# Value products over all 128 columns, narrow products kept in whole groups, bias strips through DRAM and a shorter reciprocal root in a two-block forward pass

## The chip, the cores and the metric

The kernel runs on one core of a Trainium2 chip. The metric is the device time of one execution in microseconds (us); of three runs the median counts. The engines are TensorE (PE in the profile, with PEld for its weight loads), VectorE (DVE), ScalarE (ACT), GpSimd (POOL) and SyncE (SP), which here only issues transfers. ACT issues transfers too, and such an issue stands in ACT's own stream of instructions.

## The reference

256 tokens of width 1024 pass through two blocks of two layers each. The change touches the attention of the first block:

```
diff heads (4, two maps each):  p = softmax(q k / 8 + bias, causal);  a = p0 - lam * p1;  out = a @ v  (v: 128 wide)
moba heads (8, one own block):  p = softmax(q k / 8 + bias, causal);  out = p @ v                       (v: 64 wide)
bias[i, j] = rel_bias[bucket(i - j), head]      # depends on i - j alone
rms_norm(x) = x / sqrt(mean(x * x) + 1e-6) * g   # in both blocks, of x, q, k and the heads' outputs
```

The second block (gated linear attention, attention, convolution, gates) uses the same root and the same sums of squares, and six parts of its modulation (a vector times a 1024 x 3072 matrix) are computed by TensorE with 32 wide products inside the stages of the first block.

## The kernel before, in words

Activations lie transposed, 128 channels on the partitions and 256 tokens along the free axis. Each weight arrives from DRAM as `raw` tiles of 128 x 1024 and is split by ACT into `wH` (rounded to the matmul's fp32r) and by DVE into `wL` (the rest). A projection is three fp32r products (high by high, high by low, low by high), 256 columns each in block one. The plain fp32 products of the sums and of the attention weights with the values stand as two records each in the trace.

Nothing is issued in the order in which it is written. `Rec.record` (line 212) notes each operation with its dependences, and `Rec.order` (line 271) plays them through with a cost and a latency per operation and fixes the order for every engine. At each step it takes the engine that can start first, and on it the ready operation that was written first. All instructions therefore carry line 442, where they are emitted, and tiles are told apart by name.

The parts that the change touches:

- `gsum` (line 621) adds up squares over the partitions: up to four products of 32 output columns, each on its own 32 partitions of one PSUM tile (`ms<-xsq`, `ms<-qsq`, `ms<-osq`, `ms<-gsq`, `ms<-ksq`). `mod_part` (line 688) uses two such groups of four, of 512 columns, on the modulation weights (`x<-wada,cs`). `nc.after` makes all of a group ready at the same moment, but another operation that becomes ready may still be put between them.
- `rsqrt` (line 598) computes 1/sqrt on DVE from a shifted integer start and three Newton steps: 12 dependent instructions on tiles of 1 to 16 columns (`s<-s`), 13 where a scale follows. There are 42 of them.
- `bias_strips` (line 755) makes `brow`, 12 heads by 384 distances, in SBUF. `bias_strip` (line 768) spreads the row of each head over the partitions, shifted by one per partition, into a `strip` tile: 12 transfers of 128 KB issued by ACT, each reading from one partition of `brow` in 128 runs of 1 KB.
- `attn_scores` (line 815) adds the strip to the scores (`sb<-x,s,strip` on DVE), takes the row maximum and the exponential with its sum.
- `moba_pair` (line 971) handles two 64 wide heads per tile `a`: it transposes the weights (`x<-ck,sb`), copies them (`at` on ACT) and multiplies with the head's own 64 columns of `v`. Both heads' results lie in one PSUM tile `po`, head 0 on partitions 0 to 63 and head 1 on 64 to 127, and one ACT and one DVE instruction split `po` into `Y` (`y<-x`). `x` in the trace is any PSUM tile of the attention.

`attention1` runs two diff pairs and two moba pairs per layer. Each pair needs its scores' operand `ks`, which comes from a chain: squares, `gsum`, root, a spread copy (`wide`), transposes on PE, `k` on DVE, `ks` on ACT and DVE. PE executes its instructions in the fixed order, so a `x<-ks,qh` whose `ks` is late stops all that stands behind it.

Of the kernel before, what the change touches and what calls it, by code (L numbers as in the profile page):

```python
# [20 lines left out]
P = 128  # L21
# [6 lines left out]
NEG = -1.0e30  # L28
MAGIC = 0x5F3759DF
AHEAD = {"ps": 12, "T": 16, "Q": 14}  # L30
ROLES = {"mm": 4, "x4": 4, "ms": 3, "raw": 4, "H": 7, "L": 7, "ada": 4}
# [43 lines left out]
class Op:  # L75
    __slots__ = ("i", "eng", "fn", "args", "kw", "cost", "lat", "prio", "deps", "succ", "nd", "ready", "start", "end",
                 "new", "uses", "dma", "table", "alloc")

# [53 lines left out]
class Rec:  # L132


    def __init__(self, tc):
        self.tc, self.nc = tc, tc.nc
        nc = tc.nc
        self.vector, self.scalar, self.tensor = _Proxy(self, "DVE", nc.vector), _Proxy(self, "ACT", nc.scalar), _Proxy(self, "PE", nc.tensor)
        self.gpsimd, self.sync = _Proxy(self, "POOL", nc.gpsimd), _Proxy(self, "SP", nc.sync)
        self.ops, self.tiles, self.caps, self.psum, self.acc, self.role = [], {}, {}, set(), {}, {}  # L140
        self.seen, self.old = {}, set()
        self.offset = 0.0
        self.ahead, self.rolecap = {}, {}
        self.after = None

    def pool(self, ctx, name, bufs, **k):
# [16 lines left out]
    def box(self, ap):  # L163
        pat = ap.ap
        ps, pn = pat[0]
        ps = ps or 1
        p0, f0 = divmod(ap.offset, ps) if pn > 1 or ps > 1 else (0, ap.offset)
        f1 = f0 + 1
        for s, c in pat[1:]:
            f1 += s * (c - 1)  # L170
        return p0, p0 + pn, f0, f1
# [40 lines left out]
    def record(self, eng, method, fn, args, kw):  # L212
        o = Op()
        o.i, o.eng, o.fn, o.args, o.kw = len(self.ops), eng, fn, args, kw
        o.prio = o.i + self.offset
        out = kw["out"] if "out" in kw else args[0]
        outs = [out] + ([kw["accum_out"]] if kw.get("accum_out") is not None else [])
# [53 lines left out]
    def order(self):  # L271
# [74 lines left out]
        done = 0  # L346
        total = len(ops)
        while done < total:
            best = None
            for e in engs:  # L350
                t0 = t_eng[e]
                while future[e] and future[e][0][0] <= t0:
                    r, p, i = heapq.heappop(future[e])
                    heapq.heappush(avail[e], (p, i))
                if avail[e]:
# [9 lines left out]
            s, e = best  # L365
            t_eng[e] = max(t_eng[e], s)
            while future[e] and future[e][0][0] <= s:
                r, p, i = heapq.heappop(future[e])
                heapq.heappush(avail[e], (p, i))
            p, i = heapq.heappop(avail[e])  # L370
            o = ops[i]
# [43 lines left out]
            for j in o.succ:  # L415
# [8 lines left out]
                if q.nd == 0:  # L424
                    push(q)
            for tn in o.uses:
                left[tn] -= 1
# [20 lines left out]
class Emit:  # L448
# [149 lines left out]
    def rsqrt(self, src, n, scale=None, shape=None, guard=None, more=None):  # L598
        nc = self.nc
        tiles = [self.small(n) for _ in range(5)] + [self.small(n, I32)]  # L600
        v, y, t, u, r, h = tiles
        sh = (lambda q: q) if shape is None else (lambda q: q.rearrange(shape[0], **shape[1]))
        bits = lambda q, dt: q.bitcast(dt)
        if more is not None:
# [11 lines left out]
        if scale is not None:  # L616
            nc.vector.tensor_scalar(r, y, scale, None, ALU.mult)
            return tiles[4]
        return tiles[1]
# [68 lines left out]
    def mod_part(self, l, part, after):  # L688
# [4 lines left out]
        for kk in range(0, KT, 2):  # L693
# [5 lines left out]
            if kk % 4:  # L699
                nc.after = nc.last(raw)  # L700
                for g in range(4):
                    nc.tensor.matmul(ps[32 * g:32 * g + 32, :], self.cs[:, kk - 2 + g, :], ws[g], start=kk < 4, stop=kk >= 4)
                nc.after = None
                ws = []
# [50 lines left out]
    def bias_strips(self):  # L755
# [9 lines left out]
        self.strip = [None] * 6  # L765
        self.brow = row

    def bias_strip(self, i, after):

        nc = self.nc  # L770
        st = self.t2("strip")
        nc.after = after
        for a in range(2):
            src = self.brow[2 * i + a:2 * i + a + 1, 0:T]
# [3 lines left out]
        self.strip[i] = st.rearrange("p (a b) -> p a b", a=2)  # L778

# [35 lines left out]
    def attn_scores(self, pr, a, qg, kn, rq, rcol, head):  # L815
# [10 lines left out]
        for m in range(2):  # L826
# [5 lines left out]
            for t in range(2):  # L832
                nk = P * (t + 1)
                sl = slice(t * P, t * P + nk)
                nc.vector.scalar_tensor_tensor(sb[:, sl], ps[:, t * T:t * T + nk], rq[:, rcol(m, t):rcol(m, t) + 1],
                                               st[:, T - nk:T], ALU.mult, ALU.add)
                nc.vector.tensor_reduce(mx[:, t:t + 1], sb[:, sl], AX.X, ALU.max, negate=True)
# [133 lines left out]
    def moba_pair(self, pr, qg, kn, r, v, Y):  # L971
        nc = self.nc
        for a in range(2):
# [3 lines left out]
            for m in range(2):  # L977
# [4 lines left out]
                at = self.attn_transpose(s)  # L982
                o = po[m * 64:(m + 1) * 64, :]
# [833 lines left out]
def constants():  # L1817
# [30 lines left out]
    for lv in range(7):  # L1848
# [3 lines left out]
        masks[:, lv, :] = (seg[:, None] == seg[None, :]) & (half[:, None] != half[None, :])  # L1852
    return {"ck": ck, "oneh": oneh.astype(np.float32), "maskr": np.ascontiguousarray(maskr.astype(np.float32)),
            "masks": masks.reshape(P, 7 * P).astype(np.float32)}
# [25 lines left out]
```

## Time and profile before

| | us |
|---|---|
| median of 3 runs (2056.23 to 2058.48) | 2057.44 |
| the profiled execution | 2054.4 |
| its span, first to last instruction | 2052.6 |
| PE busy (share of the span) | 2027.0 (99%) |
| PEld busy | 1847.7 (90%) |
| DVE busy | 1464.4 (71%) |
| ACT busy | 1167.6 (57%) |
| mean DMA rate | 143 GB/s |

The profile is of one execution. A PE record's length overlaps the next record's, so the cost of a piece of PE work is read from the starts in the timeline: a 256 column fp32r product follows the one before after 0.12 us. Waits name the engine and tile that came last by the profile.

### The profile page before, as it was taken

Reading aid. Unit: us, or ns where it says so; the run is one execution under the profiler, and the core shown is the slowest. Engines: PE = TensorE matmul, PEld = TensorE weight load, DVE = VectorE, ACT = ScalarE, POOL = GpSimd, SP = SyncE. Lnnn points to the kernel's source line nnn. Section 1 sums busy time; section 2 is a strip of 40 time slices with the busy share of each in tenths; the row PEclk is TensorE's granted clock in tenths of the full one; section 3 lists DMA queues with packets and bytes.
Section 4 is the critical chain, followed back from the end, with each engine's and each line's share of the span. In section 5 each row is a group of like instructions: output and inputs, shape, how many; then the busy total and the mean of one; then the engine's idle time right before and its main releaser. Section 6 shows DMA issues by size and latency. Waiting matters only on the chain.

```text
span 2052.6 us, 35592 instructions
## 1 busy us (share of the span) xinstructions
PE 2027.0 (99%) x14158; PEld 1847.7 (90%) x14158; DVE 1464.4 (71%) x2846; ACT 1167.6 (57%) x2055; POOL 8.7 (0%) x20
## 2 busy tenths in 40 slices
PE   9989999999999999999999999999999999999998
PEld 7879999989999989988888888888888999999997
DVE  7778986888866699983477755563467888696663
ACT  6656656767665767762366323333357777575542
POOL 0000000000000000000000000000000000000000
PEclk9999999999999999999999999999999999999999
DMA  9765665555555121232122543342361225436551
GB/s 296 140 166 200 225 226 174 185 175 175 206 185 196 60 74 64 72 120 86 53 72 72 193 135 122 115 140 96 135 214 67 89 83 186 141 116 215 176 190 68
DMA packets 86846, 292.68 MB, mean 143 GB/s; under 512 B 9452, under 2 KB 17176, under 8 KB 86424
## 3 DMA queue, kind: packets, MB, share of 16 engines
q1 hardware_dynamic: 81544, 281.50, 39.6%
q10 hardware_dynamic: 5136, 8.91, 2.8%
q8 instruction: 111, 1.82, 0.4%
q14 instruction: 55, 0.45, 0.1%
HBM read 282.51 MB, written 4.19 MB: 140 GB/s over the span
## 4 chain that ended last, share of the span: by engine, by line
PE 97%; DMA 1%; DVE 1%; ACT 0%; issue 0%; ACTq 0%; SPq 0%; DVEq 0%
PE mm L442 78%; PE x L442 11%; PE acc L442 6%; PE ms L442 2%; DMA strip<-brow 1%; DVE s L442 0%; DMA xx<-in_xt_dram 0%; ACTq L442 0%; ACT h L442 0%; DVE wL L442 0%; DVE sb L442 0%; ACT y L442 0%; ACT wH L442 0%; ACT xg L442 0%; DVE h L442 0%
## 5 line engine op out<-in xcount | busy, mean ns | idle before, releaser
L442 DVE TENSOR_TENSOR wL<-raw,wH 128x1024 fp32r<-128x1024 f32 (+1 forms) x472 | 569.7, 1217 | 307.0 <-PE mm L442 144.6
L442 ACT ACTIVATE wH<-raw 128x1024 fp32r<-128x1024 f32 (+1 forms) x472 | 491.5, 1053 | 252.2 <-DVE wL L442 112.0
L442 PE MATMUL mm<-h2H,wH 128*128 128x256 f32 (+1 forms) x1504 | 504.2, 338 | 2.1 <-ACT h2H L442 2.1
L442 PE MATMUL mm<-h2L,wH 128*128 128x512 f32 (+2 forms) x1504 | 504.0, 337 | 0.0
L442 PE MATMUL mm<-h2H,wL 128*128 128x256 f32 (+1 forms) x1472 | 497.5, 338 | 0.0
L442 PEld LDWEIGHTS mm<-h2H,wH 128*128 128x128 f32 x1504 | 283.6, 190 | 33.2 <-issue 3.5
L442 PEld LDWEIGHTS mm<-h2L,wH 128*128 128x128 f32 (+1 forms) x1504 | 283.2, 189 | 28.7 <-issue 1.6
L442 PEld LDWEIGHTS mm<-h2H,wL 128*128 128x128 f32 x1472 | 279.3, 190 | 28.6 <-issue 1.0
L442 PE MATMUL mm<-h,wH 128*128 128x256 f32 x1216 | 219.6, 283 | 0.0
L442 PEld LDWEIGHTS mm<-h,wH 128*128 128x128 f32 x1216 | 189.6, 192 | 0.0
L442 PE MATMUL mm<-h,wL 128*128 128x256 f32 x608 | 172.0, 283 | 0.0
L442 PE MATMUL mm<-xg,wH 128*128 128x256 f32 x704 | 133.9, 289 | 1.5 <-ACT wH L442 1.5
L442 PE MATMUL acc<-hid,wH 128*128 128x256 f32 x704 | 128.2, 284 | 0.0
L442 PEld LDWEIGHTS mm<-h,wL 128*128 128x128 f32 x608 | 116.7, 192 | 0.0
L442 PEld LDWEIGHTS mm<-xg,wH 128*128 128x128 f32 x704 | 112.1, 195 | 4.0 <-ACT wH L442 1.9
L442 PE MATMUL mm<-xL,wH 128*128 128x512 f32 (+1 forms) x320 | 111.4, 348 | 0.0
L442 PE MATMUL mm<-xH,wL 128*128 128x512 f32 (+1 forms) x320 | 111.2, 348 | 0.0
L442 PE MATMUL mm<-xH,wH 128*128 128x512 f32 (+1 forms) x320 | 111.0, 348 | 0.0
L442 PEld LDWEIGHTS acc<-hid,wH 128*128 128x128 f32 x704 | 109.8, 192 | 0.8 <-issue 0.8
L442 PE MATMUL mm<-xg,wL 128*128 128x256 f32 x352 | 101.6, 290 | 0.2 <-DVE wL L442 0.2
L442 PE MATMUL acc<-hid,wL 128*128 128x256 f32 x352 | 98.4, 283 | 0.0
L442 ACT ACTIVATE gt<-mm,hb 128x512 f32<-128x512 f32 (+1 forms) x48 | 27.8, 579 | 116.1 <-PE mm L442 116.0
(295 smaller groups left out, 3850.5 us busy)
## 6 DMA issues: line engine op xcount, KB each, us to landing
raw<-in_w_dram SPq DMA_DIRECT2D x272, 512.0 KB, 3.7
raw<-in_w1up_dram SPq DMA_DIRECT2D x88, 512.0 KB, 4.1
wada<-in_wada_dram SPq DMA_DIRECT2D x48, 512.0 KB, 5.4
raw<-in_w1in_dram SPq DMA_DIRECT2D x46, 512.0 KB, 5.9
raw<-in_w1dn_dram SPq DMA_DIRECT2D x44, 512.0 KB, 4.4
raw<-in_w1out_dram SPq DMA_DIRECT2D x16, 512.0 KB, 4.5
crow<-in_crow_dram SPq DMA_DIRECT2D x6, 512.0 KB, 6.4
qh<-qh SPq DMA_DIRECT2D x16, 128.0 KB, 2.2
```

Source lines behind the costliest of these rows:

```text
L442: o.fn(*o.args, **o.kw)
```

## The change

1. `moba_pair`: the product of a head's weights takes the values of both heads, 128 columns, into its own half of `po`'s free axis, and the 64 rows of the head itself are read. The one ACT and one DVE instruction per tile become two each, on 64 partitions.
2. `gsum` and `mod_part` mark all but the first product of a group with `join`. When `order` has placed an operation and the next one in the text is so marked and ready, it is placed at once, whatever else is ready.
3. `bias_strips` stores `brow` to a DRAM tile by SP. `bias_strip` is one transfer by SP for two heads, 256 KB, 256 runs of 1 KB read from DRAM with a step of one element per partition. The constant tables are mirrored for that, and `attn_scores` reads the strip backwards, with a step of -1.
4. `rsqrt`: no shift (the halving is a product with -0.5 on the integer read as a number), one third-order step and one Newton step, with the scale folded in: 9 instructions.

```diff
     def gsum(self, ps, sqs, ones, start=True, stop=True):
         nc.after = max(nc.last(sq) for sq in sqs)
         for g, sq in enumerate(sqs):
+            nc.join = g > 0
             nc.tensor.matmul(ps[32 * g:32 * g + 32, :self.free(sq)], self.c(ones), sq, start=start, stop=stop)
-        nc.after = None
+        nc.after, nc.join = None, False
...
+            if must is not None:
+                e, i = ops[must].eng, must
+                p, s = ops[i].prio, max(t_eng[e], ops[i].ready)
+                gone.add(i)
+                must = None
...
+            if o.i + 1 < total and ops[o.i + 1].join and ops[o.i + 1].nd == 0:
+                must = o.i + 1
...
-        nc.vector.tensor_scalar(h, bits(tiles[0], I32), 1, None, ALU.logical_shift_right)
-        nc.vector.tensor_scalar(bits(tiles[1], I32), h, -1, MAGIC, ALU.mult, ALU.add)
-        for i in range(3):
-            nc.vector.tensor_tensor(out=t, in0=y, in1=y, op=ALU.mult)
-            nc.vector.scalar_tensor_tensor(u, t, -0.5, v, ALU.mult, ALU.mult)
-            nc.vector.scalar_tensor_tensor(y, u, 1.5, y, ALU.add, ALU.mult)
+        nc.vector.tensor_scalar(y.bitcast(I32), v.bitcast(I32), -0.5, MAGIC, ALU.mult, ALU.add)
+        nc.vector.tensor_tensor(out=t, in0=y, in1=y, op=ALU.mult)
+        nc.vector.tensor_tensor(out=w, in0=t, in1=v, op=ALU.mult)
+        nc.vector.scalar_tensor_tensor(w, w, RQ[1], w, ALU.add, ALU.mult)
+        nc.vector.scalar_tensor_tensor(y, w, RQ[2], y, ALU.add, ALU.mult)
+        nc.vector.tensor_tensor(out=t, in0=y, in1=y, op=ALU.mult)
+        nc.vector.scalar_tensor_tensor(w, t, -0.5 * f * RQ[0] ** 2, v, ALU.mult, ALU.mult)
+        nc.vector.scalar_tensor_tensor(r, w, 1.5 * f, y, ALU.add, ALU.mult)
...
-        self.brow = row
+        self.brow = nc.dram_tile(self.tc, [12, 384], "brow")
+        nc.sync.dma_start(self.brow, row)
...
-            win = bass.AP(tensor=src.tensor, offset=src.offset + P - 1, ap=[list(src.ap[0]), [-1, P], [1, T]])
-            nc.scalar.dma_start(st[:, a * T:(a + 1) * T], win)
+        win = bass.AP(tensor=src.tensor, offset=src.offset + 1, ap=[[1, P], [384, 2], [1, T]])
+        nc.after = max(after, self.bstore)
+        nc.sync.dma_start(st, win)
...
+                e = st[:, nk - 1:nk]
+                bias = bass.AP(tensor=e.tensor, offset=e.offset, ap=[list(e.ap[0]), [-1, nk]])
...
-                vc = slice(a * P + m * 64, a * P + (m + 1) * 64)
-                nc.tensor.matmul(o[:, 0:T], v[:, 0, vc], at[:, 0:T], start=True, stop=False)
-                nc.tensor.matmul(o[:, P:T], v[:, 1, vc], at[:, T:T + P], start=False, stop=True)
+                o, vs = po[:, m * T:(m + 1) * T], slice(a * P, (a + 1) * P)
+                nc.tensor.matmul(o, v[:, 0, vs], at[:, 0:T], start=True, stop=False)
+                nc.tensor.matmul(o[:, P:T], v[:, 1, vs], at[:, T:T + P], start=False, stop=True)
...
-            nc.scalar.activation(hi, po[:, :T], AF.Copy)
-            nc.vector.tensor_tensor(out=lo, in0=po[:, :T], in1=hi.bitcast(F32), op=ALU.subtract)
+            for m in range(2):
+                own = slice(m * 64, (m + 1) * 64)
+                o = po[own, m * T:(m + 1) * T]
+                nc.scalar.activation(hi[own], o, AF.Copy)
+                nc.vector.tensor_tensor(out=lo[own], in0=o, in1=hi[own].bitcast(F32), op=ALU.subtract)
```

What `order` makes of it, first on PE in the first diff pair of layer 0. `x_122` and `x_119` are the modulation part's PSUM tile, `ms_224` the sums of squares of the second pair's q and k, `x2` two equal rows in a row. Before:

```order
L442 MATMUL x_122_202<-wada_204,cs 32x512 x2
L442 MATMUL x_122_202<-wada_205,cs 32x512
L442 MATMUL x_92_172<-ck,sb_163 128x128 x3
L442 MATMUL x_122_202<-wada_205,cs 32x512
L442 MATMUL x_122_202<-wada_206,cs 32x512 x2
L442 MATMUL mm_247<-wH_218,xg_84 128x256
L442 MATMUL mm_247<-wL_219,xg_84 128x256
L442 MATMUL mm_247<-wH_218,xg_84 128x256 x2
L442 MATMUL ms_224<-qsq_225,ck 32x256
L442 MATMUL x_94_174<-at_173,v_158 128x256
L442 MATMUL x_94_174<-at_173,v_158 128x128
L442 MATMUL ms_224<-qsq_225,ck 32x256
```

With the change:

```order
L462 MATMUL mm_246<-wL_222,xg_84 128x256
L462 MATMUL ms_224<-qsq_225,ck 32x256 x2
L462 MATMUL ms_224<-qsq_226,ck 32x256 x2
L462 MATMUL x_119_202<-wada_203,cs 32x512 x2
L462 MATMUL x_119_202<-wada_204,cs 32x512 x2
L462 MATMUL x_119_202<-wada_205,cs 32x512 x2
L462 MATMUL x_119_202<-wada_206,cs 32x512 x2
L462 MATMUL ms_232<-ck,rows_231 128x128 x2
```

Three broken groups stand there as whole ones, twelve narrow products in a row.

The second place is where the strips of the first moba pair are fetched, on ACT before and on SP now. Before, on ACT:

```order
L442 ACTIVATE rows_321<-ms_314 128x256
L442 ACTIVATE wH_335<-raw_334 128x1024
L442 ACTIVATE wH_372<-raw_371 128x1024
L442 DMA strip_339<-brow_97 128x1x256 x2
L442 DMA strip_340<-brow_97 128x1x256 x2
L442 ACTIVATE wH_375<-raw_374 128x1024
L442 ACTIVATE wH_379<-raw_378 128x1024
L442 ACTIVATE v_338<-mm_337,rs_113 128x256
```

With the change, on SP (`qh` is the copy of the scaled q to the other half of the partitions):

```order
L462 DMA qh_316<-qh_316 64x512 x2
L462 DMA raw_378<-in_w1in_dram 128x1024
L462 DMA raw_398<-in_w1out_dram 128x1024
L462 DMA raw_401<-in_w1out_dram 128x1024
L462 DMA strip_336<-brow 128x2x256
L462 DMA strip_337<-brow 128x2x256
L462 DMA raw_439<-in_w1out_dram 128x1024
```

The four transfers have left ACT's stream; two of twice the size stand on SP between weight loads.

The third place is on PE, ahead of the second pair's scores in layer 0, with the change (before, 32 products of 256 columns stood between `wide` and `ks`):

```order
L462 MATMUL ms_238<-ck,wide_239 128x128 x4
L462 MATMUL x_108_191<-at_190,v_159 128x256
L462 MATMUL x_108_191<-at_190,v_159 128x128
L462 MATMUL ms_161<-osq_176,ck 32x128 x2
L462 MATMUL ms_161<-osq_192,ck 32x128 x2
L462 MATMUL ms_195<-ck,rows_194 128x128
L462 MATMUL mm_304<-xg_84,wH_241 128x256 x2
L462 MATMUL mm_304<-xg_84,wL_242 128x256
L462 MATMUL mm_304<-xg_84,wH_241 128x256 x2
L462 MATMUL x_167_250<-ks_230,qh_228 128x256
```

Less work stands now between the transposes that give `k` its factor and the scores that need `ks`.

## Rows read from the trace of the kernel before

**Rows 1.** The page: the chain that ended last, shares of the span by engine.
```profile
PE 97%; DMA 1%; DVE 1%; ACT 0%; issue 0%; ACTq 0%; SPq 0%; DVEq 0%
```

**Rows 2.** PE's waits from 90 to 142 us: us in total, times, longest.
```profile
PE x L442 <- DVE sb L442: 3.8, 3, 2.1
PE x L442 <- issue: 3.8, 1, 3.8
PE mm L442 <- DVE wL L442: 1.1, 2, 0.8
PE x L442 <- PE mm L442: 0.7, 1, 0.7
PE x L442 <- ACT at L442: 0.6, 1, 0.6
PE mm L442 <- ACT wH L442: 0.2, 1, 0.2
```

**Rows 3.** Timeline of ACT (ACTq: its queue issuing): start, length, what, idle before it.
```profile
84.29 5.18 ACTq L442 DMA_DIRECT2D strip<-brow  x1
89.56 2.01 ACT L442 ACTIVATE wH<-raw 128x1024 fp32r<-128x1024 f32 x2 [6.86 <-issue]
...
113.19 8.31 ACTq L442 DMA_DIRECT2D strip<-brow  x3
```

**Rows 4.** The tile strip, over the span: durations in ns, and landing.
```profile
L442 DVE SCALAR_TENSOR_TENSOR sb<-x,s,strip x64: 327/406/477, 39.1 to 459.8; 128x128 f32<-128x128 f32 x32, 128x256 f32<-128x256 f32 x32
L442 ACTq DMA_DIRECT2D strip<-brow x12: 528/620/5177, 31.3 to 116.3; - x12
...
DMA to landing us min/median/max: 7.1/11.6/18.6
```

**Rows 5.** Stretches: length, busy time per engine, granted clock, DMA share, GB/s.
```profile
97.00:100.00 3.00, 3.00 (x17) 3.00 (x16) 3.00 (x11) 1.54 (x8) 0.00 (x0) 0.50 0.81 70
454.00:468.00 14.00, 13.64 (x98) 11.36 (x96) 12.01 (x34) 8.04 (x24) 0.00 (x0) 1.00 0.23 76
```

**Rows 6.** DMA issues: count, KB each, median us to landing.
```profile
wd<-in_wd_dram SPq DMA_DIRECT2D x8, 128.0 KB, 4.1
```

**Rows 7.** Timeline of PE: a 128 wide value product, a narrow one, two narrow ones.
```profile
55.28 0.82 PE L442 MATMUL x<-at,v 128*128 128x256 f32 x4
...
56.05 0.40 PE L442 MATMUL mm<-wH,xg 128*128 128x256 f32 x2
...
106.03 0.28 PE L442 MATMUL mm<-xg,wH 128*128 128x256 f32 x1
106.24 0.86 PE L442 MATMUL x<-at,v 128*64 128x256 f32 x4
...
107.26 0.28 PE L442 MATMUL mm<-xg,wL 128*128 128x256 f32 x1
...
442.95 0.88 PE L442 MATMUL x<-at,v 128*64 128x256 f32 x8
```

**Rows 8.** Timeline of PE: groups of 32 wide products, whole (x8) and in pieces.
```profile
24.36 0.64 PE L442 MATMUL ms<-qsq,ck 128*32 128x256 f32 x8
...
44.69 1.90 PE L442 MATMUL x<-wada,cs 128*32 128x512 f32 x10
...
70.14 1.04 PE L442 MATMUL x<-wada,cs 128*32 128x512 f32 x2
...
71.59 1.06 PE L442 MATMUL x<-wada,cs 128*32 128x512 f32 x8
```

**Rows 9.** PE's waits over the whole span: us in total, times, longest.
```profile
PE mm L442 <- ACT h2H L442: 2.1, 2, 1.9
...
PE ms L442 <- DVE s L442: 1.3, 1, 1.3
```

**Rows 10.** Timeline of DVE after the last matmul: the last root, first and last row.
```profile
2045.80 0.15 DVE L442 SCALAR_TENSOR_TENSOR s<-s 128x1 f32<-128x1 f32 x1
...
2048.10 1.42 DVE L442 SCALAR_TENSOR_TENSOR y<-og,s,xt 128x512 f32<-128x512 f32 x2
```

More of the change, by code (lines that the diff above doesn't have):

```diff
@@ L29 @@
 MAGIC = 0x5F3759DF
+RQ = (0.3755374238926038, -3.334362783627379, 4.997213710402795)
 AHEAD = {"ps": 12, "T": 16, "Q": 14}
@@ L76 @@
     __slots__ = ("i", "eng", "fn", "args", "kw", "cost", "lat", "prio", "deps", "succ", "nd", "ready", "start", "end",
-                 "new", "uses", "dma", "table", "alloc")
+                 "new", "uses", "dma", "table", "alloc", "join")
 class _Proxy:
@@ L144, in __init__ @@
         self.after = None
+        self.join = False
     def pool(self, ctx, name, bufs, **k):
@@ L169, in box @@
         for s, c in pat[1:]:
-            f1 += s * (c - 1)
+            if s < 0:
+                f0 += s * (c - 1)
+            else:
+                f1 += s * (c - 1)
         return p0, p0 + pn, f0, f1
@@ L215, in record @@
         o.prio = o.i + self.offset
+        o.join = self.join
         out = kw["out"] if "out" in kw else args[0]
@@ L347, in order @@
         total = len(ops)
+        must = None
+        gone = set()
         while done < total:
@@ L351, in order @@
                 t0 = t_eng[e]
-                while future[e] and future[e][0][0] <= t0:
+                while future[e] and (future[e][0][0] <= t0 or future[e][0][2] in gone):
                     r, p, i = heapq.heappop(future[e])
                     heapq.heappush(avail[e], (p, i))
+                while avail[e] and avail[e][0][1] in gone:
+                    heapq.heappop(avail[e])
                 if avail[e]:
@@ L365, in order @@
             s, e = best
[L366 to L370, printed above, removed]
+            if must is not None:
+                e, i = ops[must].eng, must
+                p, s = ops[i].prio, max(t_eng[e], ops[i].ready)
+                gone.add(i)
+                must = None
+            else:
+                t_eng[e] = max(t_eng[e], s)
+                while future[e] and future[e][0][0] <= s:
+                    r, p, i = heapq.heappop(future[e])
+                    if i not in gone:
+                        heapq.heappush(avail[e], (p, i))
+                p, i = heapq.heappop(avail[e])
             o = ops[i]
@@ L599, in rsqrt @@
         nc = self.nc
-        tiles = [self.small(n) for _ in range(5)] + [self.small(n, I32)]
-        v, y, t, u, r, h = tiles
+        v, y, t, w, r = tiles = [self.small(n) for _ in range(5)]
         sh = (lambda q: q) if shape is None else (lambda q: q.rearrange(shape[0], **shape[1]))
-        bits = lambda q, dt: q.bitcast(dt)
         if more is not None:
@@ L701, in mod_part @@
                 for g in range(4):
+                    nc.join = g > 0
                     nc.tensor.matmul(ps[32 * g:32 * g + 32, :], self.cs[:, kk - 2 + g, :], ws[g], start=kk < 4, stop=kk >= 4)
-                nc.after = None
+                nc.after, nc.join = None, False
                 ws = []
@@ L765, in bias_strips @@
         self.strip = [None] * 6
-        self.brow = row
+        self.brow = nc.dram_tile(self.tc, [12, 384], "brow")
+        nc.sync.dma_start(self.brow, row)
+        self.bstore = len(nc.ops) - 1
     def bias_strip(self, i, after):
         nc = self.nc
[L771 to L774, printed above, removed]
-            win = bass.AP(tensor=src.tensor, offset=src.offset + P - 1, ap=[list(src.ap[0]), [-1, P], [1, T]])
-            nc.scalar.dma_start(st[:, a * T:(a + 1) * T], win)
+        st = self.t2("strip").rearrange("p (a b) -> p a b", a=2)
+        src = self.brow[2 * i:2 * i + 1, 0:T]
+        win = bass.AP(tensor=src.tensor, offset=src.offset + 1, ap=[[1, P], [384, 2], [1, T]])
+        nc.after = max(after, self.bstore)
+        nc.sync.dma_start(st, win)
         nc.after = None
-        self.strip[i] = st.rearrange("p (a b) -> p a b", a=2)
+        self.strip[i] = st
     def lam(self, l, init):
@@ L834, in attn_scores @@
                 sl = slice(t * P, t * P + nk)
+                e = st[:, nk - 1:nk]
+                bias = bass.AP(tensor=e.tensor, offset=e.offset, ap=[list(e.ap[0]), [-1, nk]])
                 nc.vector.scalar_tensor_tensor(sb[:, sl], ps[:, t * T:t * T + nk], rq[:, rcol(m, t):rcol(m, t) + 1],
-                                               st[:, T - nk:T], ALU.mult, ALU.add)
+                                               bias, ALU.mult, ALU.add)
                 nc.vector.tensor_reduce(mx[:, t:t + 1], sb[:, sl], AX.X, ALU.max, negate=True)
```

9 lines of the change are left out of this document (3 added, 6 removed).

## The prediction

> **What bounds the kernel now.** I read the page's chain first: 97% of the span is PE's own instructions [rows 1]. So only two things can shorten this kernel: PE instructions that cost less, and stretches in which PE stands. The second list is short. From 90 to 142 us PE's waits add up to 3.8 + 3.8 + 1.1 + 0.7 + 0.6 + 0.2 = 10.2 us [rows 2], and all of it is in the two moba pairs of layer 0. The timeline of ACT says why: an issue of a strip transfer keeps ACT for up to 5.18 us, ACT's next activation at 89.56 comes after 6.86 us in which it stood, and from 113.19 three such issues take 8.31 us [rows 3]. Behind them wait the copies that make `ks`, so PE waits for scores; the "issue" wait of 3.8 us is this one. A strip lands after 11.6 us in the median, 18.6 at worst [rows 4], and that is the other 3.8 us, in which `sb` waits for its bias. After the wait of 3.8 us, during which PE did nothing, the granted clock is 0.50 from 97 to 100 us, the lower level of 1.2 GHz [rows 5]: 3 us of work at half speed, 1.5 us lost.
>
> Of the PE work itself the timeline shows what a switch between widths costs. I count from start to start, in slots of 0.12 us for a usual product.
>
> **Value products.** A 128 wide pair of products starts at 55.28, and the second usual product behind it starts at 56.05: 0.77, less one slot, is 0.65 us. A narrow pair follows a product that starts at 106.03 and ends its slot at 106.15; the second usual product behind starts at 107.26: 1.11 less a slot is 0.99 us [rows 7]. So a narrow pair, 0.86 long in its row, costs 0.13 more than its length, and widening saves 0.34. Of the 16 narrow pairs, 12 stand alone: 12 x 0.34 = 4.1 us. Two more are joined to sums and counted there. The last two stand side by side, and both heads together take 0.88 [rows 7], with the switch 1.01 against 2 x 0.65: this place loses 0.3. **Term 1: -3.8 us.**
>
> This is where a rule speaks against the change. The Trainium skill, TensorEngine Tiling (Array Packing), Key Properties, says that tiles operate independently, different ones in parallel, and that a change of the mode drains the engine. By its first half the narrow products of two heads should cost one, and widening them would lose at every pair of heads. The row at 442.95 agrees, but only one of eight pairs of heads stands so in the order; the other rows show its second half.
>
> **Whole groups.** A piece costs its length plus the same 0.13. The sums' whole group of eight records is 0.64 long, so 0.77. A piece of two records of the modulation's group is 1.04 long, a run of eight 1.06 [rows 8]: both cost about 1.19, however few products stand in it. A second group right behind adds the difference of 1.90 and 1.06 [rows 8], 0.84. So each split costs a run. In the diff pairs of layer 0 the order shows three runs of modulation pieces where two groups stood and two runs for two others, and a sum split in two; now every group is whole. What falls away is 1.19 twice and 0.77 once, and 0.3 net where groups now stand next to each other: 3.4 us. Layer 1 has two split modulation groups whose ends stand in a run with other groups (0.84 each) and two split sums (0.7 each): 3.1 us. The third pair of layer 0 has a split sum around a narrow value pair: 0.8. The split at the end of layer 0 of block two I count at nothing: behind it PE waits 1.9 us for `h2H` [rows 9], and the chain on DVE and ACT sets that end. **Term 2: -7.3 us.**
>
> **Strips.** ACT loses its 12 issues. SP gets one store of `brow` and six transfers, each in front of weight loads. No row shows this transfer. The nearest is `wd`: 128 KB from DRAM in 256 runs, landing after 4.1 us [rows 6]; a strip is 256 runs twice as long. The other end is that it lands as late as now, 11.6 us [rows 4]. I take some 5 us, nearer to `wd`, since the 1 KB runs come from DRAM and no longer out of one partition. In the order the pairs' strips stand one to three loads behind the place where ACT issued them or ahead of it, and well ahead of `sb`, apart from the first, which is needed at 39.1 [rows 4] as soon as it lands; 1 us there is covered by products that need no strip. SP's later loads are pushed back by two short issues. So the 10.2 us of waits and the 1.5 us of the clock go. What is late next is the softmax chain itself: in layer 1, where no strip is fetched, the same stretch of 14 us has PE busy for 13.64 [rows 5]. I leave 1.2 us for that in the two pairs. **Term 3: -10.5 us**, and between 0 and -11.7 by the two ends.
>
> **Shorter roots.** 42 roots lose three instructions each. The last one, after the last matmul, takes from 2045.80 to 2048.10 for 12 [rows 10]: 0.19 each, so 0.6 at the very end, where nothing covers it. Of the others PE waits only for those that end a wait: 1.3 us for `s` [rows 9], where two roots share DVE and 1.0 should go, and 1.9 for `h2H`, with two roots in its chain, 1.2. The rest is hidden by products. **Term 4: -2.8 us.** Below nothing a shorter chain can't cost on the path.
>
> **What is added.** `Y` is split in two halves per tile: eight instructions more on ACT and on DVE. They wait for both heads' products as before, so at the end of each layer's last pair, where `mm<-y` waits, one ACT instruction of some 0.3 us is added: 0.6. The backward read of the strip changes no count; no row shows a step of -1, and I cost it at nothing, as both kinds read one value per lane and position, up to twice the 0.41 us at the other end (a rival below). In the second pair of layer 0 only some 2 us of PE work is left between the transposes for `k` and the scores; a chain over ACT lies between the two, so I put one more wait there, of the size of one that PE shows in this stretch, 0.7 [rows 2]. **Term 5: +1.3 us.**
>
> **Sum.** -3.8 - 7.3 - 10.5 - 2.8 + 1.3 = -23.1. The 11.1 us of terms 1 and 2 lie in attention stages where DVE is nearly as full as PE: 12.01 of 14 us from 454 to 468 [rows 5]. PE will come to some places before its operands; I take a fifth off, 2.2. That leaves -20.9. The profiled execution took 2054.4, so 2033.5 by its own time; it lies 3.0 under the median of the runs, and I take the same off the median: 2057.4 - 20.9 = **2036.5 us**.
>
> **Rivals.** *The strips stay late, on SP.* For it: the runs are still 1 KB, there are 256 in one transfer, and an issue can hold a queue for 5.18 us [rows 3], now with all weights behind it. Against it: `wd` lands in 4.1 [rows 6]. Term 3 is gone then, 2036.5 + 10.5 = 2047, and 2049 with weights late. Chance 0.10. The Trainium skill, DMA: Bandwidth & Descriptors, Issuing engines are not separate DMA queues, says that another issuing engine only saves the time to initiate a transfer, usually small beside the transfer. By that rule the move to SP gives nothing, and the source has to; the 5.18 us in the row are against its "usually small".
>
> *DVE and ACT set the pace.* PE is 11.1 us shorter in stages where DVE has 2 of 14 us free [rows 5]. If half of terms 1 and 2 turns into waits instead of a fifth, 3.3 more is lost, and with new waits for `sb` and `ks` of a few us 2040 to 2046; I write 2043. Against it: DVE loses three root steps per root in the same stages, and ACT its strips. Chance 0.20.
>
> *The backward read is slow.* The other side: 64 instructions `sb`, 0.41 us in the median [rows 4], all ahead of the softmax. If each takes twice as long and nothing covers it, 26 us come on top: 2063. It is slower than before from 20.9 / 64 = 0.33 us more each. Chance 0.04.
>
> *Narrow pairs side by side.* If, by the tiling rule above, the narrow products of all eight pairs of heads overlapped before, term 1 would be 8 x 0.3 = +2.4 instead of -3.8, and the time 2043. The timeline contradicts it for seven of eight. Chance 0.02.
>
> That `join` does nothing can be excluded: the new order has no split group.
>
> **How the numbers follow.** The forecast has 0.58, as 2030 to 2041: without the fifth and the 1.2 us left over, and with the 1.2 us of the split in block two, the sum is about -27, and 2029 leaves a little for the order elsewhere. Below 2029 I see 0.06. The range reaches up to 2049 to take in the first, second and fourth rival. Outside are the backward read and the tail below: 0.10, with little more above 2049. A measurement of this kernel can tell about 0.2%, 4.1 us, from no change. Faster than 2053.3 are all cases but the backward read and a strip case that goes worse than I priced it: 0.93. Between, 0.03; slower than 2061.5, 0.04.
>
> **What would show it.** In the new profile no narrow value product is left, every group of sums has eight records in a row, and PE's busy time falls by about 11 us to 2016. No DMA issue stands on ACT in the attention, PE's waits in the two moba pairs are below 2 us, and no stretch there is at 0.50 of the clock. Strips land in under 6 us. `sb` keeps its 0.41. The last root takes 1.7 us. The prediction is wrong if PE's busy time falls but its waits rise by as much, if `sb` waits for a strip issued by SP, or if `sb` grows.

## The result and the profile after

| | before | changed |
|---|---|---|
| median of the runs | 2056.84 us (2055.74 to 2058.48) | 2032.87 us (2032.69 to 2035.09) |
| ratio | | 0.9885, 95% interval 0.9868 to 0.9902 |
| span of the profiled execution | 2052.6 us | 2031.0 us |
| PE busy / PE idle in the span | 2027.0 / 25.6 us | 2014.2 / 16.8 us |

The change saves 24.0 us by the medians and 21.6 us by the two profiled executions. I forecast 20.9. Of the 21.6, PE's busy time gives 12.8 and its idle time 8.8.

The page of the changed kernel: busy time of each engine, and the chain that ended last.

```profile
PE 2014.2 (99%) x14158; PEld 1846.4 (91%) x14158; DVE 1447.8 (71%) x2720; ACT 1171.4 (58%) x2063; POOL 8.6 (0%) x20
...
PE 92%; ACT 0%; DVE 0%; DMA 0%; issue 0%; DVEq 0%; ACTq 0%
```

The profile follows this chain back only to 130.2 us, so its 92% says nothing of most of layer 0's attention. That PE sets the pace there too rests on its busy time, 99% of the span, and on its waits. PE's waits of the changed kernel from 60 to 142 us (us in total, times, longest), to be held against [rows 2]:

```profile
PE mm L462 <- ACT y L462: 1.0, 2, 0.9
PE ms L462 <- ACT rows L462: 0.6, 1, 0.6
PE x L462 <- DVE sb L462: 0.2, 1, 0.2
PE mm L462 <- DVE y L462: 0.2, 1, 0.2
```

Of 10.2 us of waits 2.0 are left in a longer window, and only 0.2 of them is for `sb`. The tile `strip` of the changed kernel (durations in ns, first and last start, landing), against [rows 4]:

```profile
L462 DVE SCALAR_TENSOR_TENSOR sb<-x,s,strip x64: 324/405/478, 46.1 to 441.1; 128x128 f32<-128x128 f32 x32, 128x256 f32<-128x256 f32 x32
L462 SPq DMA_DIRECT2D strip<-brow x6: 377/426/965, 35.6 to 101.8; - x6
...
DMA to landing us min/median/max: 4.6/5.6/7.7
```

A transfer twice as large lands in half the time. The backward read costs nothing: `sb` takes 0.405 us in the median where it took 0.406. The stretch that ran at half the clock in [rows 5], in the changed kernel:

```profile
97.00:100.00 3.00, 3.00 (x26) 2.92 (x25) 2.31 (x5) 2.92 (x8) 0.00 (x0) 1.00 0.22 52
```

The clock is granted in full and 26 products start where 17 did. The DMA engines are busy for 0.22 of the time instead of 0.81, but no strip is in flight there now, and the 70 GB/s of before were in part weights. What strips from one partition do by themselves shows in a stretch of the kernel before in which all packets are theirs:

```profile
89.00:92.00 3.00, 2.78 (x24) 2.58 (x22) 0.00 (x0) 2.44 (x4) 0.00 (x0) 1.00 0.81 26
```

They keep the DMA engines busy for 0.81 of the time and move 26 GB/s.

PE's groups of whole and split products, with shapes apart (busy us, mean ns of one, then idle before), first of the kernel before, then of the changed one:

```profile
L442 PE MATMUL x<-wada,cs 128*32 128x512 f32 x96 | 17.3, 601 | 0.0
...
L442 PE MATMUL ms<-qsq,ck 128*32 128x256 f32 x96 | 10.3, 390 | 0.0
```

```profile
L462 PE MATMUL x<-wada,cs 128*32 128x512 f32 x96 | 12.3, 598 | 0.0
...
L462 PE MATMUL ms<-qsq,ck 128*32 128x256 f32 x96 | 7.7, 391 | 0.0
```

The same number of instructions, of the same length each, takes 7.6 us less, since more of them run side by side. The last root on DVE, against [rows 10]:

```profile
2025.00 0.15 DVE L462 SCALAR_TENSOR_TENSOR s<-s 128x1 f32<-128x1 f32 x1
...
2026.73 1.41 DVE L462 SCALAR_TENSOR_TENSOR y<-og,s,xt 128x512 f32<-128x512 f32 x2
```

It takes 1.73 us instead of 2.30.

### The profile page after: what moved, and what is told of

The parts are those of the page before. It is cut to its first block, busy times and chain, and to the rows that moved or that the text cites. A ratio compares the mean times of both kernels' runs of the same rounds, so it can differ in the third digit from the quotient of the medians.

```text
span 2031.0 us, 35501 instructions
## 1 busy us (share of the span) xinstructions
PE 2014.2 (99%) x14158; PEld 1846.4 (91%) x14158; DVE 1447.8 (71%) x2720; ACT 1171.4 (58%) x2063; POOL 8.6 (0%) x20
## 4 chain that ended last, share of the span: by engine, by line
PE 92%; ACT 0%; DVE 0%; DMA 0%; issue 0%; DVEq 0%; ACTq 0%
PE mm L462 75%; PE x L462 10%; PE acc L462 6%; PE ms L462 2%; DMA raw<-in_w_dram 0%; DVE y L462 0%; DVE s L462 0%; ACT y L462 0%; DVE wL L462 0%; ACT h L462 0%; ACT wH L462 0%; ACT fH L462 0%; ACT att L462 0%; DVE og L462 0%; ACT F L462 0%
```

## The experiments

Two theories stood against each other. **Terms that add**: each part is worth what its rows say, alone or in company. **One stall in front of the others**: while strips come out of one partition, the rest can't show what it saves in layer 0. Inside them were three smaller questions: whether a strip's source or its queue matters, whether the width of the value products or the number of switches matters, and whether DVE and ACT set the pace. All times are medians of runs beside runs of the kernel before on the same chip.

Two things limit what small differences can say. First, the changed kernel was not run again beside the later runs: its 2032.87 us were measured beside 2056.84 for the kernel before, theirs beside 2057.33 or 2057.86. Taken as ratios to the kernel before, the differences to the changed kernel come out up to 1.5 us smaller when a part is taken out, and up to 1 us better for the two kernels with the heads together. Second, up to the first sum of q's squares all the kernels run the same instructions in the same order, and even so that sum starts anywhere from 24.22 to 26.12 us in the profiled executions. The changed kernel and the one whose groups may be split:

```profile
24.30 0.64 PE L462 MATMUL ms<-qsq,ck 128*32 128x256 f32 x8
...
25.64 0.64 PE L447 MATMUL ms<-qsq,ck 128*32 128x256 f32 x8
```

So a difference of 1 to 2 us between two profiled executions is no effect by itself.

### One part alone

**Wide value products alone.** The kernel before with this part:

```
-                nc.tensor.matmul(o[:, 0:T], v[:, 0, vc], at[:, 0:T], start=True, stop=False)
...
+                nc.tensor.matmul(o, v[:, 0, vs], at[:, 0:T], start=True, stop=False)
...
+            for m in range(2):
+                own = slice(m * 64, (m + 1) * 64)
```

> The kernel before with the 128 wide value products and the split of Y alone. Terms as predicted: -3.8 + 0.6 for the split of Y, so -3.2 us. Switch cost undersized: counted to the third usual product behind instead of the second, a lone narrow pair costs 0.50 more than a wide one (the profile of the change has 0.573 + 0.03 + 0.20 where the one of before has 0.09 + 0.795 + 0.20 + 0.22), so 12 x 0.50 less 0.2 at the place with two pairs side by side, less 0.6: about -5. DVE and ACT set the pace: half of term 1 turns into waits, -1.3 or nothing. Narrow products of two heads overlapped before: +2.4.

Measured: 2058.35 against 2058.19 us, ratio 1.0003 (0.9994 to 1.0011). No gain. The planner, with other costs to work from, now split the modulation's groups further: 17 pieces stand in the trace where before has 14. The row shows what that costs:

```profile
L442 PE MATMUL x<-wada,cs 128*32 128x512 f32 x96 | 18.5, 602 | 0.0
```

18.5 us instead of 17.3, which is 1.2 of the 3.2 that I had forecast: in part, a saving at one place was paid at another by the order. The profiled execution also has 10.2 us at 0.50 of the clock from 80 to 155 us where that of before has 3.4. What took the rest of the gain is not settled.

**Whole groups alone.**

```
+                    nc.join = g > 0
                     nc.tensor.matmul(ps[32 * g:32 * g + 32, :], ...
...
+            if o.i + 1 < total and ops[o.i + 1].join and ops[o.i + 1].nd == 0:
+                must = o.i + 1
```

> The kernel before with whole groups of narrow products alone. Terms as predicted: -7.3 us. DVE and ACT set the pace: about half, -3.6, with PE's busy time down by 7 and its waits up by 3 to 4. Groups that were split only around narrow value products stay next to them, so some switches remain: -5.

Measured: 2053.87 against 2058.19 us, 4.3 less, ratio 0.9980 (0.9972 to 0.9989). PE's busy time falls from 2027.0 to 2021.7, but its waits from 90 to 146 us grow to 13.4. The largest two:

```profile
PE ms L457 <- ACT rows L457: 7.7, 1, 7.7
PE mm L457 <- DVE wL L457: 3.3, 1, 3.3
```

`rows` is a copy on ACT. ACT's timeline (ACTq: its queue issuing) has it behind three issues of strips:

```profile
109.08 8.93 ACTq L457 DMA_DIRECT2D strip<-brow  x3
118.11 1.06 ACT L457 ACTIVATE wH<-raw 128x1024 fp32r<-128x1024 f32 x1 [8.45 <-issue]
119.08 0.36 ACT L457 ACTIVATE rows<-ms 128x256 f32<-128x256 f32 x1
```

It is not the work of DVE or ACT that set the pace there, but this one queue: the groups saved PE's time, and PE then stood for it. The half clock took more as well: in the stretches at 0.50 PE lost 4.5 us of its busy time between the first sum of q's squares and the end, where the kernel before lost 1.7.

**Strips through DRAM alone.**

```
+        nc.sync.dma_start(self.brow, row)
...
-            nc.scalar.dma_start(st[:, a * T:(a + 1) * T], win)
...
+        win = bass.AP(tensor=src.tensor, offset=src.offset + 1, ap=[[1, P], [384, 2], [1, T]])
...
+        nc.sync.dma_start(st, win)
```

> The kernel before with brow in DRAM, strips fetched by SP and the backward read of the strip alone. Terms as predicted: -10.5 us, PE's waits in the two moba pairs of layer 0 from 10.2 to about 1 us, and no stretch at 0.50 of the clock. The strips' wait was only the first of several chains: the softmax chain takes its place, -5 to -7, with waits for sb and ks of a few us left. Strips late on SP: 0.

Measured: 2045.55 against 2058.19 us, 12.6 less, ratio 0.9943 (0.9929 to 0.9957). Between the two profiled executions it is 9.4 (spans of 2043.2 and 2052.6). From 90 to 146 us PE waits 0.3 us for `at` and 0.2 for `y`, and for nothing else. No softmax chain took the strips' place.

**Short roots alone.**

```
-        for i in range(3):
...
+        nc.vector.scalar_tensor_tensor(w, w, RQ[1], w, ALU.add, ALU.mult)
+        nc.vector.scalar_tensor_tensor(y, w, RQ[2], y, ALU.add, ALU.mult)
```

> The kernel before with the shorter root alone. Terms as predicted: -2.8 us (0.6 behind the last matmul, 1.0 at the wait for s, 1.2 at the wait for h2H). Hidden but for the end: -0.6. DVE sets the pace in the attention: 42 roots of 0.5 us would show there as well, -5 or more.

Measured: 2056.26 against 2058.19 us, ratio 0.9994 (0.9985 to 1.0003): 1.9 less, not told from nothing. The waits for `s` of 1.3 and for `h2H` of 1.9 [rows 9] are gone, as forecast, but in layer 0 others grew, and the modulation fell into 18 pieces in the trace (18.1 us). PE's largest wait there:

```profile
PE x L444 <- DVE ks L444: 10.3, 2, 7.2
```

### One part left out of the changed kernel

**Strips as before.**

```
-        nc.sync.dma_start(st, win)
...
+            nc.scalar.dma_start(st[:, a * T:(a + 1) * T], win)
```

> The changed kernel with the strips of before, issued by ACT from one partition. Additive by the run with the strips' part alone (-12.6 against before): 2033 + 12.6 = 2045.5. If the strips' stall eats what the other parts save in layer 0 (the waits in its moba pairs grew from 10 to 13 us with whole groups alone and with short roots alone), then 2049 to 2053, with PE's waits there of 12 us or more, and layer 1's stage as short as in the changed kernel. Strips worth 10.5: 2043.

Measured: 2050.34 us (2047.78 to 2053.16), 17.5 over the changed kernel. With the other three parts in place the strips cost 17.5, alone they gave 12.6 (17.5 and 9.4 between profiled executions): the second theory. PE's largest wait from 60 to 146 us, and three stretches (length, busy times, clock, DMA share, GB/s):

```profile
PE x L459 <- DVE ks L459: 7.2, 1, 7.2
```

```profile
95.00:98.00 3.00, 1.88 (x9) 1.88 (x10) 2.91 (x5) 1.93 (x2) 0.00 (x0) 0.50 0.80 27
...
128.00:131.00 3.00, 3.00 (x16) 3.00 (x15) 2.98 (x10) 1.38 (x6) 0.00 (x0) 0.50 0.94 143
...
140.00:143.00 3.00, 3.00 (x14) 2.82 (x13) 2.56 (x4) 1.66 (x3) 0.00 (x0) 0.50 0.41 160
```

PE's idle time is 27.5 against 16.8 us, and its busy time 2021.0 against 2014.2. The second is the clock: in these stretches PE runs at the lower of its levels, 1.2 GHz, and does the same work longer. Before the change there was one such stretch in layer 0 [rows 5], here there are three. From 80 to 155 us, taken in steps of 3 us, PE's busy time times the share of the clock that was not granted adds up to 6.9 us, as much as its busy time grew. Not every stall does this. The kernel before stands for 6.4 of the 18 us from 122 to 140 in shorter waits and keeps its clock throughout; the stretch with most waiting:

```profile
128.00:131.00 3.00, 1.20 (x11) 0.99 (x9) 2.25 (x10) 1.97 (x8) 0.00 (x0) 1.00 0.95 137
```

**Groups that may be split.**

```
-                    nc.join = g > 0
```

> The changed kernel without the rule that keeps groups whole: 19 pieces of the sums for q and k where 16 groups are, 14 of the modulation where there are 10. Terms as predicted: +7.3, 2040. Additive by the run with whole groups alone: +4.3, 2037. By pieces: 3 of 0.8 and 4 of 1.19, +7.2.

Measured: 2040.94 us (2040.31 to 2041.25), 8.1 over the changed kernel. The modulation's row is back at 17.5 us and that of the sums at 8.9, together 6.4 over the changed kernel. The 6.4 are the surer figure: by the ratios to the kernel before the difference is 7.0 instead of 8.1, and the profiled execution of this run was already 1.3 behind at the first sum of q's squares.

**Narrow value products, Y in one piece.**

```
-                o, vs = po[:, m * T:(m + 1) * T], slice(a * P, (a + 1) * P)
+                o = po[m * 64:(m + 1) * 64, :]
+                vc = slice(a * P + m * 64, a * P + (m + 1) * 64)
```

> The changed kernel with the narrow value products of before and Y in one piece. Against the changed kernel's 2032.9: terms as predicted, +3.2, so 2036. Switch cost counted to the third product: +5, so 2038; the groups are whole in both, so the splits that hid the gain when the products alone were widened (16 modulation pieces where before has 14) are not there. Widening is worth nothing: 2033. Narrow products overlap by themselves: 2030.5.

Measured: 2034.52 us (2033.81 to 2035.82), 1.6 over the changed kernel. The runs of the two overlap, and 0.9 of the 1.7 us between the profiled executions lie ahead of the first sum of q's squares, so the 1.6 is not told from nothing. In the profiles PE is busy 3.1 us longer (2017.3) and idle 1.4 us less (15.4). So widening saves some 3 us of PE work there, and gives half of it or more back at the layers' ends, where PE waits for `y` (2.2 us in the changed kernel, 0.5 here).

**Long roots.**

```
-        nc.vector.scalar_tensor_tensor(y, w, RQ[2], y, ALU.add, ALU.mult)
...
+        for i in range(3):
```

> The changed kernel with the root of 12 or 13 instructions. Terms as predicted: +2.8, 2035.7, with 0.6 of it behind the last matmul and waits of 1.3 for s and 1.9 for h2H back. Additive by the run with the roots alone: +1.9, 2034.8. If the strips' stall hid more in that run (outside layer 0's attention its stages were shorter by 4.2 and its attention in layer 1 longer by 1.2 with three modulation pieces more): +4, 2037.

Measured: 2039.45 us (2038.89 to 2039.80), 6.6 over the changed kernel and more than any of the three expectations. PE's waits show both that I had named, `h2H` and `s`:

```profile
PE mm L460 <- ACT h2H L460: 2.1, 2, 1.9
...
PE ms L460 <- DVE s L460: 1.3, 1, 1.3
```

PE's idle time is 3.3 us longer, the tail behind the last product 0.6 of it. Its busy time is 2.8 longer. 1.7 of that is the clock, at 0.50 from 1534.6 to 1538.1 us, right behind the wait of 1.9 for `h2H`. The kernel before has the same wait and keeps its clock there, so it is open why it fell here. The modulation stands in eleven pieces instead of ten, but its row is only 0.2 longer (12.5). About 1 us stays open.

### The strip: source or queue

**From DRAM, issued by ACT.**

```
-        nc.sync.dma_start(st, win)
+        nc.scalar.dma_start(st, win)
```

> The changed kernel with the strips from DRAM as there, six transfers, but issued by ACT instead of SP. If the source decides: 2032 to 2035, each issue under 1 us on ACT and each landing in 4 to 8 us. If the queue decides (an issue of so many runs holds the engine that makes it, and on ACT that holds the copies): 2045 to 2050, with PE waiting for ks and rows, as where the strips come from one partition.

Measured: 2032.89 us (2032.30 to 2034.79), the changed kernel's time. Its tile `strip`:

```profile
L462 ACTq DMA_DIRECT2D strip<-brow x6: 366/388/632, 39.0 to 105.1; - x6
...
DMA to landing us min/median/max: 4.0/4.9/6.1
```

**From one partition, issued by SP.** Strips as before, with

```
-            nc.scalar.dma_start(st[:, a * T:(a + 1) * T], win)
+            nc.sync.dma_start(st[:, a * T:(a + 1) * T], win)
```

> The changed kernel with the strips from one SBUF partition, forward, twelve transfers, as before, but issued by SP. If the source decides: landing 7 to 19 us as before, SP's queue held up to 5 us at an issue, weights late behind it; sb waits and wH waits, 2040 to 2050. If it was enough to take the issues from ACT: 2033 to 2036, though the strips land as late as before.

Measured: 2054.54 us (2053.43 to 2055.91), 21.7 over the changed kernel, above what either expectation allowed and worse than on ACT. Its tile `strip`, PE's largest wait, and SP's timeline (start, length, what):

```profile
L459 SPq DMA_DIRECT2D strip<-brow x12: 560/886/5435, 31.1 to 117.2; - x12
...
DMA to landing us min/median/max: 8.2/12.5/17.6
```

```profile
PE x L459 <- DVE sb L459: 18.7, 3, 10.0
```

```profile
75.04 9.47 SPq L459 DMA_DIRECT2D strip<-brow  x4
84.61 4.89 SPq L459 DMA_DIRECT2D raw<-in_w1in_dram  x1
```

The source decides. With strips from DRAM the queue is worth nothing; with strips from one partition SP is worse than ACT by 4.2 us (2050.34 there), as PE waits longer for `sb`. An issue from one partition held ACT for 5.18 us [rows 3] and holds SP for up to 5.4; one from DRAM holds ACT for 0.39 in the median and 0.63 at most. The long ones are the third and fourth of four in a row (2.2 to 2.8 and 5.3 to 5.4 us on SP, the first two 0.6 to 1.2), and a weight load from DRAM right behind them holds SP for 4.89 as well. So the hold looks like a backlog and not like the price of one issue; that was not tried. What about that source is slow stays open too: it differs in several things, SBUF instead of DRAM, one partition of it, windows that step down by one from partition to partition, and twelve transfers instead of six. I didn't try them apart.

### The value products: width or switches

**Narrow, both heads side by side.** The changed kernel with narrow products and Y in one piece, the four products of two heads kept together:

```
+            for t in range(2):
+                for m in range(2):
+                    nc.join = t + m > 0
+                    o = po[m * 64:(m + 1) * 64, :]
+                    vc = slice(a * P + m * 64, a * P + (m + 1) * 64)
+                    nc.tensor.matmul(o[:, t * P:T], v[:, t, vc], ats[m][:, t * T:T + t * P], start=t == 0, stop=t == 1)
```

> The changed kernel with narrow value products (Y in one piece), those of both heads put side by side as one whole group of four. By the row of before with two narrow pairs side by side (0.81 from start to the next start, with 0.09 ahead and some 0.3 behind) such a group costs about as much as two lone wide pairs (0.56 each over their neighbours' slots): 2033, within 1 us of the changed kernel, and 5 better than the narrow pairs alone. What decides is then how often the width changes, not the width. If head 0's products, which now wait for head 1's softmax, cost more than they give: 2036 or more, with longer waits for y at the ends. If the width itself decides: as with lone narrow pairs, 2036 to 2038.

Measured: **2026.61 us** (2026.06 to 2028.03), ratio to the kernel before 0.9851 (0.9839 to 0.9864): 6.3 us under the changed kernel, more than I had expected of it. It beats both kernels. PE is busy for 2010.5 us, 3.7 less than in the changed kernel, and idle for 14.2, 2.6 less. PE's timeline, first with narrow products as lone pairs (the run above), then side by side:

```profile
97.99 0.86 PE L462 MATMUL x<-at,v 128*64 128x256 f32 x4
98.79 0.39 PE L462 MATMUL mm<-xg,wL 128*128 128x256 f32 x1
```

```profile
103.89 0.87 PE L462 MATMUL x<-at,v 128*64 128x256 f32 x8
104.69 0.39 PE L462 MATMUL mm<-wH,xg 128*128 128x256 f32 x1
```

Eight records take what four took, 0.80 us from start to the next start: the second head's products are free. In the sums by shape it is 8.3 us instead of 16.4:

```profile
L462 PE MATMUL x<-at,v 128*64 128x256 f32 x32 | 10.3, 404 | 0.0
...
L462 PE MATMUL x<-at,v 128*64 128x128 f32 x32 | 6.1, 273 | 0.0
```

```profile
L462 PE MATMUL x<-at,v 128*64 128x256 f32 x32 | 5.2, 404 | 0.0
...
L462 PE MATMUL x<-at,v 128*64 128x128 f32 x32 | 3.1, 273 | 0.0
```

**Wide, both heads next to each other.** The control: the changed kernel with

```
+                nc.join = m > 0
+                nc.tensor.matmul(o, v[:, 0, vs], ats[m][:, 0:T], start=True, stop=False)
+                nc.join = True
+                nc.tensor.matmul(o[:, P:T], v[:, 1, vs], ats[m][:, T:T + P], start=False, stop=True)
```

> The changed kernel with the wide value products of both heads put next to each other, as the narrow ones were in the run before. If two narrow products at once are what gave 6.3 us there (on the rows, eight records in 0.80 us, started 0.007 us apart in twos), wide ones next to each other give nothing, since they run one after the other (1.2 to 1.4 us for eight): 2032 to 2034. If keeping the heads together is what gave it (fewer switches, another order around them): 2027.

Measured: 2030.49 us (2030.12 to 2032.79), ratio 0.9869 (0.9856 to 0.9883), 2.4 under the changed kernel by the medians. That is between the two expectations. PE's busy time hardly moves (2013.9 against 2014.2), since eight wide records still take 1.23 us to the next start:

```profile
102.64 1.47 PE L462 MATMUL x<-at,v 128*128 128x256 f32 x8
103.87 0.36 PE L462 MATMUL mm<-xg,wH 128*128 128x256 f32 x1
```

The waits for `y` fall from 2.2 us to 0.3. So of the 6.3 us some 2.4 come with keeping the heads together, and 3.9 with narrow products that run two at once. The eight places account for most of the 3.9: 1.23 less 0.80 at each makes 3.4, and PE's busy time differs by 3.4 (2013.9 and 2010.5). The last 0.5 may come with Y in one piece, which the narrow run has and the wide one hasn't; that was not tried apart. The 2.4 is the less certain, as the intervals of the two ratios overlap. The Trainium skill, TensorEngine Tiling (Array Packing), Key Properties, says that different tiles can execute in parallel; the rows of the narrow products agree, eight records in 0.80 us where four took 0.80.

## Why the prediction was right, and where its sizes were off

- **PE's busy time.** Terms 1 and 2 with the clock's 1.5 made 12.6; measured 12.8. The shares fit too: from the first sum of q's squares on, the clock gave 1.7 and the work itself 10.8, against 11.1 for the two terms. **The fifth that I took off** as a guess for DVE and ACT was not there in busy time; nor did waits grow by it: terms 3 to 5 and this fifth left 8.3 us of idle time to go, and 8.8 went.
- **Term 1, value products, -3.8.** Mechanism right: PE is busy 3.1 us less by it in the profiles. With term 5's 0.6 for the halves of `Y` I forecast a net of 3.2; the net is 1.6 at most, not told from nothing, since the waits for `y` rose by 1.7. That they fall to 0.3 with the halves of `Y` kept but the heads put together speaks against the added instruction of 0.3 us which I priced, and for where the last products stand. The wait for `ks` that term 5 priced at 0.7 did not come; 0.6 stand at `rows`.
- **Term 2, whole groups, -7.3.** Measured 8.1 when taken out (6.4 in its rows), and 7.6 in the two rows of before and after. Alone it gives 4.3; the strips' stall hides the rest, as the longer waits and the half clock of that run show.
- **Term 3, strips, -10.5.** Measured 12.6 alone (9.4 between profiled executions) and 17.5 in company. The waits and the half clock of the profiled execution went as forecast. The step that missed is the one to the median: "it lies 3.0 under the median of the runs, and I take the same off the median". Those 3 us were not a fixed distance. The changed kernel's median lies 1.9 above its profiled span, that of the strips' part alone 2.4 above its own, and that of before 4.2. The profiled execution of the kernel before was an unusual one: its 2054.4 us are less than any of the other 57 runs of that kernel took (2055.17 at least), and its granted clock was 0.998, where the 53 runs with a clock on record have 0.993 to 0.997. Time goes with that clock: the three runs at 0.997 took 2055.4 us on average, the 30 at 0.994 took 2057.9. The strips decide about it: over all kernels, every other run with a clock on record has 0.991 to 0.997 with strips from one partition, and 0.997 to 0.999 with strips from DRAM. So 20.9 was right to 0.7 us for the profiled executions (21.6), and the medians differ by 24.0.
- **The first strip, costed at nothing**, was covered: SP issues it at 35.6, it and the second land within 5.5 us, and `sb` starts only at 46.1, behind three splits `wL` that keep DVE from 42.43 on. New waits stand there all the same, 0.9 us each for `sb` and `osq`, where PE had none from 25 to 60 us. The strip was there in time, so the first comes from what DVE does ahead of it; the cause of the second was not tried. Both are in the 24.0.
- **Term 4, roots, -2.8.** Both waits and the tail went as named. Taken out of the changed kernel the roots cost 6.6: 3.3 of idle time, near the term, and 2.8 of busy time that I had not counted, 1.7 of it a stretch at half clock.
- **The parts do not add.** Put in alone they give -0.2, 4.3, 12.6 and 1.9, together 18.6; taken out last they cost 1.6, 8.1, 17.5 and 6.6, together 33.8. The whole is 24.0. A stall that PE reaches earlier grows (PE's waits from 90 to 146 us are 10.2 us before, 13.4 with whole groups alone and 13.2 with short roots alone), and the planner makes another order each time. So which part gets how much of the 24.0 depends on the company it is measured in. That the sum came out near is better founded than any one term.
- **The range's lower end.** Without the fifth the sum is -23.1, and the 1.2 left over and the 1.2 of the split bring it to -25.5, not to about -27. So 2029 lay further out than the text says. It did not matter: the time is 2032.87.
- **Rivals.** Strips late on SP fell: they land in 5.6 us, and it was the source that did it (2032.9 us with strips from DRAM on either queue). The Trainium skill, DMA: Bandwidth & Descriptors, Issuing engines are not separate DMA queues, says that transfers run on the same DMA engines whichever engine starts them, and that another issuing engine saves only the time to initiate a transfer, usually small beside it. The strips from DRAM agree, 2032.9 us on either queue; those from one partition do not, as an issue held its engine for up to 5.4 us of a landing of 12.5 in the median, and SP was 4.2 us worse than ACT. DVE and ACT as the pace fell: PE's idle time fell by 8.8, and in layer 1's attention, where no strip is fetched, its waits are 1.1 us from 340 to 500, all for `y`, where the kernel before has 1.8. The slow backward read fell. Narrow pairs side by side was wrong about the order of before, as its rows said, and still the most useful rival: what those pairs could be, not what they were, gives the faster kernel. I used the row of 0.88 us only to see what the change loses there, and did not ask what it would give at all eight places.
- **What I said would show it.** No stretch in the pairs at 0.50 of the clock, waits below 2 us, busy time about 2016: as said, with waits of 1.4 us from 90 to 142 and 2014.2. Strips in under 6 us: 5.6 in the median, 7.7 at worst.

## What to carry to other kernels

When one stall stands ahead of other savings, remove it first and time the others behind it: put in alone, whole groups showed 4.3 of 8.1 us and short roots 1.9 of 6.6. Before narrow products are widened, see whether their partners can be put beside them: two products on different columns ran in the time of one, while two wide ones ran one after the other. And when an order is made by a planner, count the pieces of each group in every variant, since an edit elsewhere can split them.

## What I had not expected of the hardware

- Products on the two halves of the columns start in twos, 7 ns apart, and share their time: eight records in 0.80 us, four in 0.80.
- Transfers from one SBUF partition held whichever engine issued them (5.18 us ACT, 5.4 us SP), held the weight load behind them too (4.89 us), and kept the DMA engines busy for 0.81 of the time at 26 GB/s.
- A stall can cost twice: in the run with strips as before, three stretches of layer 0 ran at 0.50 of the clock, and PE's busy time rose by 6.8 us for the same work. But not every stall does: the kernel before stood for 6.4 us from 122 to 140 us at 1.00.
